# Later mixing splits, later gate-pair sums and a re-ordered second gate in a fused encoder-layer kernel

## Chip, core and metric

One core of a Trainium2 chip runs the whole layer as one program. The metric is the device time of one execution in microseconds (us): 1302.18 as the median of three runs before the change (1301.49 to 1302.49). Lower is better.

## What is computed

One layer of an encoder on 256 positions of width 2048, all in float32: a projection `P = RMSNorm(x) @ w_in` whose columns are gMLP u and v, attention q, k, v, and two gates; then two branches, a gated merge, an output projection, and a convolutional gated MLP. Cut to what matters here:

```python
uv, qkv, gates = split(rms_norm(x) @ w_in)
y_a = u * (w_s @ LN(v) + b)              # per 128-position chunk, 8 groups of 128 columns
y_b = neighbourhood_attn(q, k, v, rpb)   # 16 heads, learned relative bias
g_a, g_b = split(sigmoid(gates))         # 2048 columns each
merged = g_a * (y_a @ Wb_A) + g_b * (y_b @ Wb_B)
x = x + merged @ w_out
up = depthwise_conv(rms_norm(x) @ w_up)
x = rms_norm(x + (silu(gate) * val) @ w_down)
```

## The kernel before

**Products.** Every matrix product is made from values split in two: `whi` is the weight copied into a reduced format by ScalarE (L170, ACT), `wlo` is the remainder that VectorE subtracts (L171, DVE). Three matmuls (high by high, low by high, high by low; L250 to L252, or L317 to L319 in `triple`) make one product tile in a PSUM bank; there are 8 banks of 128x512.

**Pieces.** The program is a list of *pieces*, one for 256 rows of a weight block (512 columns). For each piece `begin(i)` runs in program order: it issues the DMA of piece i+4 on SyncE's queue (SP; five `wraw` buffers), lets ACT and DVE split piece i+3 (four `whi` and `wlo` buffers), and then runs the tasks that were put down for piece i with `at(i, f)`; TensorE (PE) then gets piece i's matmuls. Each engine works its own instructions off in this order, so the piece at which a task is put down decides what stands ahead of it on ACT, on DVE, on SP's queue and on GpSimd's (POOL).

**Mixings.** After each of the two groups of u columns, `mix(g)` (L690) runs at four pieces in a row: 4 matmuls with `w_s` (L693), two bias additions (L697) and a product with u (L698) on DVE. Its result `ya` (one buffer) is split by `end_mix`: ACT copies the high part (L536), DVE subtracts the low part (L537). `mix` begins with `end_mix` for the one before, and puts an `end_mix` at the next piece; that task stands behind the next `mix` of the same piece, so the second, third and fourth result of a group of four are split in the piece in which they are made. The second four run during the columns of the first q and k block (`g_at[0]`); at that block's end `combine` (L680 ACT, L682 DVE) and `spread` (L746, L747 DVE; L753 to L755 ACT) prepare the first two heads, and `attend` sends their scores to PE (L828).

**Heads.** `attend(hp, i)` spreads a pair of heads over ten pieces: scores at i, exponentials (L851, ACT) at i+1, weights (L859, ACT) at i+3, the turning of the weights on PE (L868) at i+5, their product with v (L878) at i+8. The last pair runs beside the first branch products (`g_at[8]`, `g_at[9]`).

**Wide products with sums.** The second halves of the two gates (`g_gw[0]`, `g_gw[1]`) are made by `run_wide` with a seven-product scheme: for certain pairs of pieces ("quads") 7 products in place of 8, from sums of activations and sums of weights. For a quad whose first piece is i, `wide` puts down: at i-3 the weight sums (L363, L364, L360, L361, DVE), at i-2 their split (L374 ACT, L375 DVE), at i-4 a read of the activation sums from DRAM (L1224, POOL queue). For a *kept* pair (`GATE_SPLIT`) the split weight sums were made early in the kernel and lie in DRAM; they are read back on the POOL queue (L1216) in two halves, "13" and "24", and the plain part of the pair is loaded at half width. `GATE_SPLIT[br] = {pair: (lead of the activation sums, lead of "13", lead of "24")}`. `GATE_ORDER[br]` is the order of the 16 row blocks, `GATE_QUADS[br]` says which pairs of that order are quads. Activation sums that are not at hand (`GATE_MADE`) are made by `sums_job` (L1312 and L323 to L326 on DVE; a piece later L1317 ACT and L1318 DVE; then a write to DRAM, L1322, POOL queue); for the last of them the piece is `g_at[8][1] + GATE_LATE`, and its buffer is closed after `g_m[0]`, at piece 12 of that count.

**The start of the second gate.** Its 16 pieces are called n0 to n0+15 below. The first gate's last results come off PSUM in `post_sums` (L590 to L594) and `add_sums` (L599); its sigmoid is L924 (ACT, with a table load ahead of it). At piece n0+2 `turn_m` turns a merged block on PE (L957) into two banks, which ACT (L962, L526) and DVE (L531) must empty before two of the four banks of the second gate's first quad can be written. That quad is also at n0+2, since position 0 of `GATE_QUADS[1]` is left out.

Of the kernel before, what the change touches and what calls it, by code (L numbers as in the profile page):

```python
# [50 lines left out]
X_SUMS = ((1, 5, 6), (2, 12, 13), (6, 18, 19))  # L51
GATE_KEPT, GATE_MADE = (1, 2, 6), (0, 3, 4)
GATE_QUADS = ((0, 1, 2, 4, 5, 6), (1, 2, 4, 5, 6))
GATE_ORDER = ((2, 3, 0, 1, 4, 5, 10, 11, 12, 13, 6, 7, 8, 9, 14, 15), (10, 11, 0, 1, 2, 3, 14, 15, 4, 5, 6, 7, 12, 13, 8, 9))
GATE_SPLIT = ({0: (4, 6, 5), 3: (4, 6, 6)}, {0: (4, 6, 6), 3: (4, 6, 6)})
GATE_FIRST = (40, (44, 46, 48, 48), (49, 51))
GATE_JOB = (3, (6, 6, 7, 7), (9, 12))
GATE_SUMS = ((0, 38, 40, "y4", "y5"), (3, 39, 40, "y6", "y7"))
GATE_LATE, Y_LATE = 4, 44
KEEP_AT = (22, 25, 29)  # L60
OUT_PAIRS = (0, 1, 2, 3, 4)
OUT_SUMS = (1, 3, 6, 9, 13)
# [16 lines left out]
def trunk_kernel(ctx, tc, x, x_t, vecs, w_in, ln_g, ln_b, w_st, b_s, rpb, w_branch, w_out, w_up, w_down,  # L79
# [26 lines left out]
    def bank():  # L106
        return psum.tile([128, 512], F32, name="bank")
# [81 lines left out]
    def at(i, f):  # L189
        tasks.setdefault(i, []).append(f)  # L190

    cur = [0]
# [91 lines left out]
    def wide(src, row0, order, c0, acts, quads, room, done, sums=None, stored=None, split=None, late=False):  # L284
        n0 = plan_wide(src, row0, order, c0)
        boxes = {}
        for q in quads:
            i = n0 + 2 * q
            k = order[2 * q]
            units[i], units[i + 1] = 1, 2  # L290
            b = boxes[q] = {}
            ready = split[0].get(k // 2) if split else None
            if stored:
                b["acts"] = {}
                at(i - (ready[0] if ready else 4), lambda b=b, k=k: stored(k // 2, b["acts"]))
            else:
                b["acts"] = sums[k]
            if ready:
                halved.add(i)
                for n, lead in zip(("13", "24"), ready[-2:]):  # L300
                    at(i - lead, lambda b=b, k=k, n=n: split[1](k // 2, b, n))
                continue
            whole[i] = whole[i + 1] = None
            halves = late and q == quads[0]
            at(i - 3, lambda i=i, b=b, halves=halves: weight_sums(i, b, room, halves))
            if halves:
                at(i - 2, lambda b=b: b.pop("rest")())
            at(i - 2, lambda b=b: weight_sums_split(b, room))
        return ("wide", n0, order, acts, quads, boxes, done)
# [225 lines left out]
    def split_plain(p, dst):  # L535
        nc.scalar.activation(dst[:, 0, :], p, AF.Copy)  # L536
        nc.vector.tensor_sub(dst[:, 1, :], p, dst[:, 0, :].bitcast(F32))  # L537
# [119 lines left out]
    def ev_u(j):  # L657
        def done(ps, i):
            G = gm_pool["p"]
            if j == 0:  # L660
                gm_pool["u"] = [G.tile([128, T], F32, name=f"u{b}") for b in range(8)]
            us = combine(ps)
            for b in range(4):
                nc.vector.tensor_mul(us[b], us[b], st1["rb"])

            def act():
                for b in range(4):
                    nc.scalar.activation(gm_pool["u"][j * 4 + b], us[b], AF.Gelu_apprx_tanh)

            at(i + 1, act)  # L670
            for b in range(4):
                at(i + 3 + b, lambda g=j * 4 + b: mix(g))
        return done
# [12 lines left out]
    def end_mix():  # L686
        gm_pool.pop("last", lambda: None)()

    def mix(g):
        end_mix()  # L690
        p = bank()
        for t in range(NT):
            nc.tensor.matmul(p[:, t * 128:(t + 1) * 128], gm_pool["v"][t][:, g * 128:(g + 1) * 128],  # L693
                             gm_pool["wsT"][:, g, :], start=True, stop=True)
        y = gm_pool["p"].tile([128, T], F32, name="ya", bufs=1)
        for t in range(NT):
            nc.vector.tensor_add(y[:, t * 128:(t + 1) * 128], p[:, t * 128:(t + 1) * 128], gm_pool["bs"][:, g, :])  # L697
        nc.vector.tensor_mul(y, y, gm_pool["u"][g])  # L698
        gm_pool["last"] = lambda: split_plain(y, yT[g])
        at(cur[0] + 1, end_mix)  # L700

    at_pool = {}

# [203 lines left out]
    def ev_gate_sums(br):  # L907
        def done(P, i):
            def go():
                gate_tile(br)  # L910
                mg["x", br] = [[mg["t", br][:, t, c * 512:(c + 1) * 512] for c in range(2)] for t in range(NT)]
                post_sums(P, mg["x", br], junk)

            at(i + 1, go)
        return done

    def ev_gate_wide(br):
        def done(ps, i):
            g = mg["t", br]
            add_sums(ps, mg["x", br])  # L920

            def sigmoid():
                for t in range(NT):
                    nc.scalar.activation(g[:, t, :], g[:, t, :], AF.Sigmoid, scale=st1["r"][:, t:t + 1])  # L924

            at(i + 1, sigmoid)
            for c in range(2):
                mg[br, 2 + c] = g[:, :, c * 512:(c + 1) * 512]
        return done
# [244 lines left out]
    def sums_room(name, dt):  # L1174
        return s_room["p"].tile([128, 2, 512], dt, name=name)
# [35 lines left out]
    def split_read(kept, g, tile_of):  # L1211
        def read(pair, box, n):
            u = box.setdefault("u", [])
            u.append([tile_of(pair, p + n) for p in "hl"])
            for t, src in zip(u[-1], kept[pair, g][n]):
                nc.gpsimd.dma_start(t.bitcast(F32), src)  # L1216
            if len(u) == 2:
                split_sums(box, u)
        return read

    def kept_sums(pair, box):
# [4 lines left out]

    g_gw = [wide(w_in2, 0, GATE_ORDER[br], (GA0, GB0)[br] + 1024, xt, GATE_QUADS[br], sums_room,
                 (ev_gate_sums(br), ev_gate_wide(br)), stored=kept_sums,
                 split=(GATE_SPLIT[br], split_read(g_kept, br, lambda pair, name: sums_room("k" + name, F32R))))
            for br in range(2)]  # L1230
# [41 lines left out]
    def split_rows(name, pair, g):  # L1272
        return {m: [dram.tile([128, 2, 512], F32, name=f"{name}_{h}{m}_{pair}_{g}") for h in "hl"]
                for m in ("13", "24")}
# [10 lines left out]
    for n, (pair, g) in enumerate((pair, g) for g in range(2) for pair in OUT_SPLIT[g]):  # L1285
# [3 lines left out]
                    [i + a for a in OUT_JOB[2]], 4, last=True)  # L1289
    for n, (pair, br) in enumerate((pair, br) for br in range(2) for pair in GATE_SPLIT[br]):  # L1290
        g_kept[pair, br] = split_rows("gate", pair, br)
# [261 lines left out]
```

## Time and profile before

| what | value |
|---|---|
| median of three runs | 1302.18 us |
| the profiled execution's own time | 1302.41 us |
| its span, first to last instruction | 1300.6 us |
| mean granted TensorE clock | 0.996 |
| PEld, DVE, ACT, POOL busy | 84%, 88%, 63%, 14% of the span |
| DMA: bytes, mean rate | 370.56 MB, 285 GB/s |

Rows of the profile give the line of the kernel, the engine, the operation, and `out<-in` by tile names. In a list of waits the columns are: engine and line that waited, whom for, us in total, how often, longest. In a timeline the first two columns are the start and the duration in us, and a bracket tells how long the engine had been idle and what ended that.

### The profile page before, as it was taken

What the parts mean: (1) busy time and instruction counts of PE and PEld (TensorE: products, weight loads), DVE (VectorE), ACT (ScalarE), POOL (GpSimd) and SP (SyncE); (2) the same over time, 40 slices, a digit from 0 to 9 for tenths busy, and PEclk for the clock granted to TensorE, in tenths of its full rate; (3) what the DMA queues carried; (4) which work ended last, traced back from release to release, by engine and by line L of the source; (5) the groups of instructions that cost most, each with busy time, mean ns of one, the idle gap of its engine ahead of it and who ended that gap; (6) DMA issues with size and microseconds to landing.
All of it is one profiled execution on the core that took longest, in us unless ns stands there. A gap on an engine that the chain in (4) does not pass through costs nothing.

```text
span 1300.6 us, 19691 instructions
## 1 busy us (share of the span) xinstructions
PE 1285.2 (99%) x6656; PEld 1094.2 (84%) x6656; DVE 1140.3 (88%) x1707; ACT 813.2 (63%) x1228; POOL 186.1 (14%) x336
## 2 busy tenths in 40 slices
PE   9999999999999999999999999999999999999997
PEld 7888878888788788888888888888888888888885
DVE  7898878888889788997898899899988989989988
ACT  7766577877855645466665656656565656555654
POOL 0004606334011001100001001100000001211210
PEclk9999999999999999999999999999999999999999
DMA  9789779998789876975688788789777859998993
GB/s 368 268 275 293 259 240 304 321 315 300 274 325 375 312 264 209 407 257 162 188 280 264 249 295 302 250 264 310 251 220 228 271 177 354 369 389 318 364 382 141
DMA packets 200181, 370.56 MB, mean 285 GB/s; under 512 B 16016, under 2 KB 124176, under 8 KB 200080
## 3 DMA queue, kind: packets, MB, share of 16 engines
q1 hardware_dynamic: 171728, 272.86, 61.5%
q0 software_dynamic: 27776, 95.39, 20.7%
q8 instruction: 52, 0.85, 0.3%
q10 hardware_dynamic: 576, 1.06, 0.2%
q14 instruction: 49, 0.40, 0.1%
HBM read 321.53 MB, written 45.61 MB: 282 GB/s over the span
## 4 chain that ended last, share of the span: by engine, by line
PE 64%; DVE 1%; DMA 1%; issue 0%; ACT 0%; DVEq 0%; SPq 0%
PE bank L222 24%; PE bank L226 13%; PE bank L319 8%; PE bank L317 8%; PE bank L318 8%; PE bank L251 1%; PE bank L250 1%; PE bank L252 1%; DMA wraw<-in_w_down_dram 1%; DVE wlo L171 1%; PE bank L1032 0%; DVE h L375 0%; PE bank L957 0%; DVE h L364 0%; ACT x L1158 0%
## 5 line engine op out<-in xcount | busy, mean ns | idle before, releaser
L171 DVE TENSOR_TENSOR wlo<-wraw,whi 128x1024 fp32r<-128x1024 f32 (+1 forms) x472 | 537.4, 1151 | 111.5 <-ACT whi L170 78.0
L170 ACT ACTIVATE whi<-wraw 128x1024 fp32r<-128x1024 f32 (+1 forms) x472 | 463.0, 996 | 186.6 <-PE bank L318 70.7
L222 PE MATMUL bank<-h,whi 128*128 128x512 f32 x1760 | 425.6, 392 | 0.0
L222 PEld LDWEIGHTS bank<-h,whi 128*128 128x128 f32 x1760 | 322.3, 188 | 61.6
L226 PEld LDWEIGHTS bank<-h,wlo 128*128 128x128 f32 x1760 | 225.9, 191 | 8.8
L226 PE MATMUL bank<-h,wlo 128*128 128x256 f32 x1760 | 228.7, 283 | 0.0
L1058 ACT ACTIVATE tc<-ta,ck 128x256 f32<-128x256 f32 x86 | 47.1, 595 | 110.2 <-DVE ta L1056 110.2
L317 PE MATMUL bank<-whi,h 128*128 128x512 f32 x192 | 75.5, 393 | 0.0
L319 PE MATMUL bank<-wlo,h 128*128 128x512 f32 x192 | 75.3, 392 | 0.2
L318 PE MATMUL bank<-whi,h 128*128 128x512 f32 x192 | 75.3, 392 | 0.0
L319 PE MATMUL bank<-wlo,a 128*128 128x512 f32 x188 | 73.5, 391 | 0.5 <-DVE wlo L171 0.5
L317 PE MATMUL bank<-whi,a 128*128 128x512 f32 x188 | 73.2, 390 | 0.0
L318 PE MATMUL bank<-whi,a 128*128 128x512 f32 x188 | 73.2, 389 | 0.0
L1061 DVE SCALAR_TENSOR_TENSOR tc<-ta,ck,tc 128x255 f32<-128x255 f32 x86 | 41.4, 481 | 14.4 <-ACT tc L1058 14.4
L1260 POOL DMA_DIRECT2D down_h<-so x16 | 8.7, 544 | 311.7 <-ACT so L1255 208.6
L793 POOL TENSOR_SCALAR_AFFINE_SELECT bias<-run 64x128 f32<-64x128 f32 x64 | 39.0, 642 | 90.8 <-DVE sc L836 90.1
L250 PE MATMUL bank<-whi,y 128*128 128x512 f32 x128 | 50.5, 395 | 0.0
L250 PE MATMUL bank<-whi,h 128*128 128x512 f32 x128 | 50.4, 394 | 0.0
L252 PE MATMUL bank<-wlo,h 128*128 128x512 f32 x128 | 50.0, 390 | 0.0
L252 PE MATMUL bank<-wlo,y 128*128 128x512 f32 x128 | 49.9, 390 | 0.0
L251 PE MATMUL bank<-whi,y 128*128 128x512 f32 x128 | 49.9, 390 | 0.0
L251 PE MATMUL bank<-whi,h 128*128 128x512 f32 x128 | 49.9, 390 | 0.0
(327 smaller groups left out, 2078.7 us busy)
## 6 DMA issues: line engine op xcount, KB each, us to landing
wraw<-in_w_up_dram SPq DMA_DIRECT2D x336, 256.0 KB, 4.1
wraw<-in_w_in_dram SPq DMA_DIRECT2D x107, 512.0 KB, 6.4
wraw<-in_w_down_dram SPq DMA_DIRECT2D x78, 512.0 KB, 7.7
wraw<-in_w_in_dram SPq DMA_DIRECT2D x70, 256.0 KB, 5.6
wraw<-in_w_branch_dram SPq DMA_DIRECT2D x32, 512.0 KB, 5.7
wraw<-in_w_out_dram SPq DMA_DIRECT2D x28, 512.0 KB, 5.9
h<-sums POOLq DMA_DIRECT2D x18, 512.0 KB, 7.8
tw<-in_w_down_dram POOLq DMA_DIRECT2D x8, 1024.0 KB, 9.0
```

What stands on the lines that cost most here:

```text
L170: nc.scalar.activation(h[:, k, :m], w[:, k, :m], AF.Copy)
L171: nc.vector.tensor_sub(l[:, k, :m], w[:, k, :m], h[:, k, :m].bitcast(F32))
L222: nc.tensor.matmul(p, h[:, k - k0, b * 128:(b + 1) * 128], acts(k), start=k == 0, stop=k == nk - 1)
L226: nc.tensor.matmul(p[:, :T], l[:, k - k0, b * 128:(b + 1) * 128], acts(k)[:, 0, :], start=False, stop=False)
L250: nc.tensor.matmul(p, xh, h[:, kk, :m], start=st, stop=False)
L251: nc.tensor.matmul(p, xl, h[:, kk, :m], start=False, stop=False)
L252: nc.tensor.matmul(p, xh, l[:, kk, :m], start=False, stop=sp)
L317: nc.tensor.matmul(p, xh, h, start=st, stop=False)
L318: nc.tensor.matmul(p, xl, h, start=False, stop=False)
L319: nc.tensor.matmul(p, xh, l, start=False, stop=sp)
L1058: nc.scalar.activation(v, u, AF.Identity, scale=ck[:, 1, ch:ch + 1], bias=ck[:, 3, ch:ch + 1])
L1061: nc.vector.scalar_tensor_tensor(v[:, 1:], u[:, :T - 1], ck[:, 0, ch:ch + 1], v[:, 1:], op0=OP.mult, op1=OP.add)
```

## The change

Three edits, all to what stands where; no instruction is added or taken away.

```diff
-GATE_ORDER = ((2, 3, 0, 1, ...), (10, 11, 0, 1, 2, 3, 14, 15, 4, 5, 6, 7, 12, 13, 8, 9))
-GATE_SPLIT = ({0: (4, 6, 5), 3: (4, 6, 6)}, {0: (4, 6, 6), 3: (4, 6, 6)})
+GATE_ORDER = ((2, 3, 0, 1, ...), (10, 11, 2, 3, 0, 1, 14, 15, 4, 5, 6, 7, 12, 13, 8, 9))
+GATE_SPLIT = ({0: (4, 6, 5), 3: (4, 6, 6)}, {0: (4, 7, 5), 3: (5, 4, 4)})
...
-GATE_LATE, Y_LATE = 4, 44
+GATE_LATE, Y_LATE = 7, 44
...
         gm_pool["last"] = lambda: split_plain(y, yT[g])
-        at(cur[0] + 1, end_mix)
+        if g % 4 == 3:
+            at(cur[0] + 1, end_mix)
```

The added line shifts all lines behind it by one; the rows of the changed program below carry the new numbers (L1256 for L1255, L860 for L859, and so on).

**Mixings.** Only the last `mix` of four puts down an `end_mix`; the others are split by the `end_mix` at the head of the next `mix`, one piece later. DVE, at the second four mixings (`u_1265` to `u_1267` are the u columns of groups 5 to 7, `y_1161` and `y_1162` the split results), before:

```order
L698 TENSOR_TENSOR ya<-ya,u_1265 128x256
L537 TENSOR_TENSOR y_1161<-ya,y_1161 128x256
L171 TENSOR_TENSOR wlo<-wraw,whi 128x1024
L697 TENSOR_TENSOR ya<-bank,bsb 128x128 x2
L698 TENSOR_TENSOR ya<-ya,u_1266 128x256
L537 TENSOR_TENSOR y_1162<-ya,y_1162 128x256
L171 TENSOR_TENSOR wlo<-wraw,whi 128x1024
```

and in the changed program:

```order
L698 TENSOR_TENSOR ya<-ya,u_1265 128x256
L171 TENSOR_TENSOR wlo<-wraw,whi 128x1024
L537 TENSOR_TENSOR y_1161<-ya,y_1161 128x256
L697 TENSOR_TENSOR ya<-bank,bsb 128x128 x2
L698 TENSOR_TENSOR ya<-ya,u_1266 128x256
L171 TENSOR_TENSOR wlo<-wraw,whi 128x1024
L537 TENSOR_TENSOR y_1162<-ya,y_1162 128x256
```

The subtraction L537 has changed places with the weight split L171 behind it. On ACT the copy L536 likewise now stands behind the weight copy L170 of the next piece.

**Late sums.** `GATE_LATE` moves the sums of one pair from pieces 4 and 5 to pieces 7 and 8 of `g_at[8]`. ACT, at the last pair of heads (L1255 and L170 are weight splits, L859 the weights of that pair, `pT` its turned weights), before:

```order
L1255 ACTIVATE th_3983<-tw 128x1024
L170 ACTIVATE whi<-wraw 128x1024
L1317 ACTIVATE tw<-tw 128x512
L859 ACTIVATE sc<-sc,sm 128x128 x4
L170 ACTIVATE whi<-wraw 128x1024 x2
L869 ACTIVATE pT<-bank 128x512
L170 ACTIVATE whi<-wraw 128x1024 x3
```

and in the changed program:

```order
L1256 ACTIVATE th_3983<-tw 128x1024
L170 ACTIVATE whi<-wraw 128x1024
L860 ACTIVATE sc<-sc,sm 128x128 x4
L170 ACTIVATE whi<-wraw 128x1024 x2
L870 ACTIVATE pT<-bank 128x512
L170 ACTIVATE whi<-wraw 128x1024
L1318 ACTIVATE tw<-tw 128x512
L170 ACTIVATE whi<-wraw 128x1024 x2
```

The split of the sums has gone from ahead of the heads' weights to behind the copy of the turned weights. On DVE the five instructions of the sums stand three weight splits later, and now ahead of two merge products (L935).

**Second gate.** Pairs 0 (kept) and 1 change places: the first quad, at n0+2, is now pair 1, whose weights are summed and split on the spot, and kept pair 0 comes at n0+4, two pieces later. ACT, from the first gate's post sums (`g_46..`) to the turned block (`f_..`, `m_..`), before:

```order
L590 ACTIVATE g_4625<-bank 128x512
L170 ACTIVATE whi<-wraw 128x512
L170 ACTIVATE whi<-wraw 128x1024
L170 ACTIVATE whi<-wraw 128x512
L924 ACT_TABLE_LOAD
L924 ACTIVATE g_4625<-g_4625,n_r 128x1024 x2
L170 ACTIVATE whi<-wraw 128x1024
L374 ACTIVATE h_4721<-t_4695 128x1024
L374 ACTIVATE h_4725<-t_4696 128x1024
L962 ACTIVATE f_4734<-bank 128x512
L526 ACTIVATE m_4178<-bank 128x256 x2
```

and in the changed program:

```order
L590 ACTIVATE g_4621<-bank 128x512
L170 ACTIVATE whi<-wraw 128x512
L170 ACTIVATE whi<-wraw 128x1024
L374 ACTIVATE h_4677<-t_4645 128x1024
L374 ACTIVATE h_4681<-t_4646 128x1024
L170 ACTIVATE whi<-wraw 128x512
L925 ACT_TABLE_LOAD
L925 ACTIVATE g_4621<-g_4621,n_r 128x1024 x2
L170 ACTIVATE whi<-wraw 128x1024
L963 ACTIVATE f_4734<-bank 128x512
L526 ACTIVATE m_4178<-bank 128x256 x2
```

DVE at the same place, before:

```order
L171 TENSOR_TENSOR wlo<-wraw,whi 128x512
L599 TENSOR_TENSOR g_4625<-bank,g_4625 128x512 x4
L171 TENSOR_TENSOR wlo<-wraw,whi 128x1024
L171 TENSOR_TENSOR wlo<-wraw,whi 128x512
L363 TENSOR_TENSOR t_4695<-wraw 128x512
L364 TENSOR_TENSOR t_4695<-wraw 128x512
L360 TENSOR_TENSOR t_4696<-t_4695,wraw 128x512
L361 TENSOR_TENSOR t_4696<-wraw,t_4696 128x512
L171 TENSOR_TENSOR wlo<-wraw,whi 128x1024
L375 TENSOR_TENSOR l_4722<-t_4695,h_4721 128x1024
L375 TENSOR_TENSOR l_4726<-t_4696,h_4725 128x1024
L531 TENSOR_TENSOR m_4178<-bank,m_4178 128x256 x2
```

and in the changed program:

```order
L171 TENSOR_TENSOR wlo<-wraw,whi 128x512
L363 TENSOR_TENSOR t_4645<-wraw 128x512
L364 TENSOR_TENSOR t_4645<-wraw 128x512
L360 TENSOR_TENSOR t_4646<-t_4645,wraw 128x512
L361 TENSOR_TENSOR t_4646<-wraw,t_4646 128x512
L599 TENSOR_TENSOR g_4621<-bank,g_4621 128x512 x4
L171 TENSOR_TENSOR wlo<-wraw,whi 128x1024
L375 TENSOR_TENSOR l_4678<-t_4645,h_4677 128x1024
L375 TENSOR_TENSOR l_4682<-t_4646,h_4681 128x1024
L171 TENSOR_TENSOR wlo<-wraw,whi 128x512
L171 TENSOR_TENSOR wlo<-wraw,whi 128x1024
L531 TENSOR_TENSOR m_4178<-bank,m_4178 128x256 x2
```

The four weight sums have moved ahead of the additions L599, and the splits of the weight sums (L374, L375) no longer stand right ahead of the emptying of the turned banks (L526, L531). On the POOL queue the reads of pair 0's halves are issued 7 and 5 pieces ahead of its quad, with pair 1's activation sums between them, and pair 3's halves 4 pieces ahead of its quad in place of 6, behind its activation sums.

More of the change, by code (lines that the diff above doesn't have):

```diff
@@ L53 @@
 GATE_QUADS = ((0, 1, 2, 4, 5, 6), (1, 2, 4, 5, 6))
-GATE_ORDER = ((2, 3, 0, 1, 4, 5, 10, 11, 12, 13, 6, 7, 8, 9, 14, 15), (10, 11, 0, 1, 2, 3, 14, 15, 4, 5, 6, 7, 12, 13, 8, 9))
-GATE_SPLIT = ({0: (4, 6, 5), 3: (4, 6, 6)}, {0: (4, 6, 6), 3: (4, 6, 6)})
+GATE_ORDER = ((2, 3, 0, 1, 4, 5, 10, 11, 12, 13, 6, 7, 8, 9, 14, 15), (10, 11, 2, 3, 0, 1, 14, 15, 4, 5, 6, 7, 12, 13, 8, 9))
+GATE_SPLIT = ({0: (4, 6, 5), 3: (4, 6, 6)}, {0: (4, 7, 5), 3: (5, 4, 4)})
 GATE_FIRST = (40, (44, 46, 48, 48), (49, 51))
```

## Prediction

> **What bounds the kernel now.** I read the busy shares first, then the list of TensorE's waits, then the timeline around each wait.
>
> ```profile
> PE 1285.2 (99%) x6656; PEld 1094.2 (84%) x6656; DVE 1140.3 (88%) x1707; ACT 813.2 (63%) x1228; POOL 186.1 (14%) x336
> ```
>
> ```profile
> PE bank L317 <- DVE m L531: 2.9, 1, 2.9
> ...
> PE bank L828 <- ACT ks L755: 1.4, 2, 0.9
> PE bank L868 <- ACT sc L859: 0.6, 1, 0.6
> ```
>
> PE is busy 99% of the span, so an edit that moves no product can only win what PE waits, and only these three waits lie where the change moves something. The list counts idle time alone; the timeline gives what each place costs, from the start of the last matmul ahead of it to the start of the first one behind it, against a place without a wait. The order of PE's rows there: the three products, then scores or turns, then the products again.
>
> ```profile
> 169.25 0.39 PE L252 MATMUL bank<-wlo,h 128*128 128x512 f32 x1
> ...
> 172.77 0.43 PE L250 MATMUL bank<-whi,h 128*128 128x512 f32 x1
> ```
>
> ```profile
> 220.16 0.39 PE L252 MATMUL bank<-wlo,h 128*128 128x512 f32 x1
> ...
> 221.24 0.44 PE L250 MATMUL bank<-whi,h 128*128 128x512 f32 x1
> ```
>
> Scores of the first pair of heads take 172.77 - 169.25 = 3.52 us, those of a later pair 1.08: **2.44 us** are lost.
>
> ```profile
> 331.69 0.39 PE L252 MATMUL bank<-wlo,h 128*128 128x512 f32 x1
> ...
> 332.27 0.48 PE L250 MATMUL bank<-whi,y 128*128 128x512 f32 x1
> ```
>
> ```profile
> 353.01 0.39 PE L252 MATMUL bank<-wlo,y 128*128 128x512 f32 x1
> ...
> 354.98 0.49 PE L250 MATMUL bank<-whi,y 128*128 128x512 f32 x1
> ```
>
> The turning of the last pair takes 1.97 us, that of an earlier one 0.58: **1.39 us** are lost.
>
> ```profile
> 429.61 0.39 PE L319 MATMUL bank<-kl,s 128*128 128x512 f32 x1
> 432.90 0.47 PE L317 MATMUL bank<-kh,s 128*128 128x512 f32 x1 [2.90 <-DVE m L531]
> ...
> 434.13 0.49 PE L319 MATMUL bank<-kl,s 128*128 128x512 f32 x1
> ...
> 438.01 0.40 PE L317 MATMUL bank<-whi,s 128*128 128x512 f32 x1
> ```
>
> Matmuls of 512 columns start 0.227 us apart (a triple is 0.68 us), so the step from 429.61 to 432.90 loses 3.29 - 0.23 = **3.06 us**. The ten steps from 434.13 to 438.01 take 3.88 us in place of 2.27, which loses **1.61 us** more. Why, the windows by engine say (PE, PEld, DVE, ACT, POOL busy, then the granted clock):
>
> ```profile
> 430.90:434.30 3.40, 1.40 (x6) 1.21 (x7) 3.33 (x7) 3.40 (x8) 0.39 (x1) 1.00 0.28 74
> 434.29:437.70 3.41, 3.41 (x10) 2.67 (x9) 1.76 (x3) 0.75 (x2) 2.24 (x5) 0.50 0.72 250
> ```
>
> PE was busy for 1.40 us of one stretch of 3.40, and the granted clock is 0.50 for the 3.41 us behind it. The three places together lose 2.44 + 1.39 + 3.06 + 1.61 = 8.5 us, which is all that this change can win.
>
> **The mixings.** DVE and ACT while the second four mixings run:
>
> ```profile
> 158.60 0.48 DVE L697 TENSOR_TENSOR ya<-bank,bsb 128x128 f32<-128x128 f32 x2
> 159.12 0.42 DVE L698 TENSOR_TENSOR ya<-ya,u 128x256 f32<-128x256 f32 x1
> 160.02 0.42 DVE L537 TENSOR_TENSOR y<-ya,y 128x256 fp32r<-128x256 f32 x1 [0.48 <-ACT y L536]
> 160.97 1.22 DVE L171 TENSOR_TENSOR wlo<-wraw,whi 128x1024 fp32r<-128x1024 f32 x1 [0.53 <-ACT whi L170]
> ...
> 165.63 1.41 DVE L682 TENSOR_TENSOR ta<-bank,tb 128x256 f32<-128x256 f32 x4
> ```
>
> ```profile
> 159.57 0.42 ACT L536 ACTIVATE y<-ya 128x256 fp32r<-128x256 f32 x1 [2.15 <-DVE ya L698]
> ...
> 163.09 0.42 ACT L536 ACTIVATE y<-ya 128x256 fp32r<-128x256 f32 x1 [2.15 <-DVE ya L698]
> 164.36 0.91 ACT L680 ACTIVATE tb<-bank 128x256 f32<-128x256 f32 x3
> ...
> 170.09 0.41 ACT L755 ACTIVATE ks<-ta 64x256 fp32r<-64x256 f32 x1
> ```
>
> One mixing costs 163.09 - 159.57 = 3.52 us, in which DVE works 0.48 + 0.42 + 0.42 + 1.22 = 2.54: it waits for ACT's copy of a value that it has just made, and then for the weight copy that was stuck behind that copy. A gate piece of 12 matmuls takes PE 12 x 0.227 = 2.72 us, so the two engines fall behind, and PE pays at the first scores. With the split a piece later both waits have a whole piece of other work between maker and user; the cycle falls to DVE's 2.54 us, and three of the four mixings are shortened, by 0.98 us each. L682 comes 2.9 us earlier, and with it the chain to L755: ks is ready at 170.50 - 2.9 = 167.6, and PE would ask for it at 169.25 + 0.23 = 169.48. The cover is 1.9 us for the first half of the scores and less for the second, whose copies follow on the same engine, so I take all 2.44 us; the bounds are 0 (the wait stays, if the chain is held by something else than the copies) and 2.44. The moved splits themselves cost nothing: they are the same instructions on engines with time over, and the branch products that read them (`y`) start at 332.27.
>
> **The late sums.** ACT at the last pair of heads:
>
> ```profile
> 349.38 1.04 ACT L170 ACTIVATE whi<-wraw 128x1024 fp32r<-128x1024 f32 x1
> 353.04 0.63 ACT L1317 ACTIVATE tw<-tw 128x512 fp32r<-128x512 f32 x1 [2.62 <-DVE tw L326]
> 353.58 1.27 ACT L859 ACTIVATE sc<-sc,sm 128x128 f32<-128x128 f32 x4
> ```
>
> The copy of the sums idles for DVE 2.62 us, with the heads' weights queued behind it. Without it ahead, these can run from 350.42 to 351.7, and PE asks at 353.24: the 1.39 us go, with 1.5 us of cover. Where the sums go there is work enough: their five DVE instructions then delay two L935 merges by about 2 us, but these only empty two of eight banks and the next product groups (10.9 us each) take other banks. The write to DRAM is issued later as well:
>
> ```profile
> 355.04 0.58 POOL L1322 DMA_DIRECT2D xsums<-tw  x1 [43.64 <-DVE tw L1318]
> ```
>
> It moves by three pieces of 2.7 us, to about 363, piece 10 of this count. POOL's next reads (activation sums and kept weights of the first gate, from piece 12 on) stand behind it in the queue, and one of them reuses its buffer, so that read waits until the write has landed. Its product is at piece 18, eight pieces or 22 us behind the write, which holds a write and a read of about 8 us each. I count 0; bounds 0 and 2 us lost.
>
> **The second gate.** What stands ahead of the turned banks on ACT and DVE, and DVE's emptying of them:
>
> ```profile
> 423.47 0.63 ACT L170 ACTIVATE whi<-wraw 128x512 fp32r<-128x512 f32 x1 [1.66 <-PE bank L318]
> ...
> 425.42 2.19 ACT L924 ACTIVATE g<-g,n_r 128x1024 f32<-128x1024 f32 x2
> 427.52 1.04 ACT L170 ACTIVATE whi<-wraw 128x1024 fp32r<-128x1024 f32 x1
> 428.47 1.99 ACT L374 ACTIVATE h<-t 128x1024 fp32r<-128x1024 f32 x2
> ```
>
> ```profile
> 419.31 2.48 DVE L599 TENSOR_TENSOR g<-bank,g 128x512 f32<-128x512 f32 x4
> ...
> 432.01 1.41 DVE L531 TENSOR_TENSOR m<-bank,m 128x256 fp32r<-128x256 f32 x4
> ```
>
> Now pair 1's split weight sums go earlier: the 1.99 us of L374 fall into ACT's idle 1.66 us ahead of 423.47 and push what follows by 0.33. L924 ends at 427.94, the weight copy at 428.9, its subtraction on DVE (1.22) at 430.1, and the first two L531 (0.35 apart, 0.41 long) at 430.85 in place of 432.75. PE, released 0.15 us behind that today (432.90), goes on at 431.0 where it wants to at 429.61 + 0.23 = 429.84: **a wait of 1.2 us stays**, 3.06 - 1.2 = 1.86 us go. On DVE four weight sums of the size of L599 (2.48 us) now stand ahead of L599, which delays the first gate's banks by those 2.5 us to 424.3; PE turns into them at 426.3 (429.84 less four triples and eight transposes, twice the 0.35 us of the four above). The wait's bounds are 0 (ACT gets to its table load earlier than I think) and the 3.06 of today.
>
> With 1.2 us idle, PE is busy for over 2 of any 3.4 us. Around the first scores, which lost 2.44 us in two waits, the granted clock stays 1.00, so I take the half clock as gone: 1.61 us.
>
> [...]
>
> The kept reads: pair 3's halves share buffers with pair 0's, which PE now finishes one quad (seven triples, 4.8 us) later, and they are needed at the same place.
>
> ```profile
> wraw<-in_w_in_dram SPq DMA_DIRECT2D x11, 512.0 KB, 7.9
> ...
> kl<-gate_l POOLq DMA_DIRECT2D x4, 512.0 KB, 7.2
> ```
>
> Between them lie eight triples (5.4 us), pair 2's quad (4.8) and three triples (2.0): 12 us for a landing of 7.2 (the median between 405 and 440 us). I count no wait; with a landing of 14 it would be 2.
>
> **Sum.** 2.44 + 1.39 + 1.86 + 1.61 = 7.3 us off the profiled execution's 1302.41 gives 1295.1; the median of the runs is 0.2 lower, so **1295.0**.
>
> **Rivals.**
> - *The half clock stays*, because 1.2 us idle at an unlucky place, or something else, lets it fall. Gain 5.7, time 1296.7. For it: the trace has one fall only. Against: no fall at 172 us. 0.13.
> - *Another wait takes L531's place* and nothing is won at the second gate: the copy behind the table load, or the late L599, holds the turned banks as long. Gain 3.83, time 1298.6. 0.09.
> - *The first scores still wait*, since DVE, late by its split jobs and not by the copies, comes no earlier. Gain 4.9, time 1297.5. For it: DVE is 88% busy. 0.05.
> - *Little is won anywhere*: half of the 2.44 and the 1.39, about 1300.2. The order shows that the rows did move, so this needs two failures. 0.07.
> - *Slower: the second piece of pair 1 lands late.* Its raw weights are now needed for the sums (L364) at about 420, not six us later for another pair. It is issued as
>
> ```profile
> 411.76 0.33 SPq L145 DMA_DIRECT2D wraw<-in_w_in_dram  x1
> ```
>
>   and with 7.9 us lands at 419.7. Up to about 420.6 ACT's chain covers it; every us behind that moves L599, the weight split and L531 by one. PE's wait is then 1.2 + (landing - 420.6); with the half clock's 1.61 it passes today's 4.67 plus the 3.83 won elsewhere from a landing at 426.3, 14.5 us behind the issue, and is slower by 0.2% from 428.9. At 20 us (431.8) the wait is 12.4 and the time 1302.4 + 12.4 + 1.6 - 8.5 = 1307.9. Twice the measured landing; 0.06.
>
> **Chances and range.** Forecast 0.60. About 0.2% (2.6 us) is what a measurement can tell from no change: faster by more means below 1299.6, which the forecast and the first three rivals give: 0.87; the fourth counts as the same, 0.07; slower 0.06. The range goes from 1293.4 (all 8.5 us back, 0.3 for the runs' spread) to 1298.7 (nothing at the second gate), and leaves out 0.13.
>
> **What would show it.** Right: in PE's list of waits the rows for L828 and L868 are gone, L317's is about 1.2 us, the clock is 1.00 throughout, the first scores take 1.08 us and the last turning 0.58, L536 no longer idles for L698. Wrong: a row for L828 with another releaser, a wait for L364 or L375 at the second gate, a wait of PE for `kh` or `kl`, or a stretch at 0.50 behind L317.

## The result, and the profile after

The changed kernel takes **1294.24 us** (median of four runs, 1294.04 to 1294.45), the kernel before beside it 1302.34 (1301.49 to 1303.07): ratio 0.9938, 95% interval 0.9921 to 0.9955, 8.1 us less. The profiled execution takes 1294.45 us with a span of 1292.7 and a mean granted clock of 0.998. Lines of the changed program are one higher behind L700.

The busy shares, and then TensorE's whole list of waits in the changed kernel:

```profile
PE 1282.1 (99%) x6656; PEld 1092.4 (85%) x6656; DVE 1140.8 (88%) x1707; ACT 813.8 (63%) x1228; POOL 189.1 (15%) x336
```

```profile
PE bank L493 <- DVE one L483: 1.5, 1, 1.5
PE bank L317 <- ACT m L526: 0.8, 1, 0.8
```

The shares say nothing: PE is at 99% as before. The list says it: the rows for the scores and for the last turning are gone, and the 2.9 us at the second gate have become 0.8. (Why this row names L526 and not L531 is told with the reasons below. L493 is in the start of the program, alike in both kernels.) The three places, in TensorE's timeline of the changed kernel:

```profile
169.44 0.39 PE L252 MATMUL bank<-wlo,h 128*128 128x512 f32 x1
...
170.52 0.44 PE L250 MATMUL bank<-whi,h 128*128 128x512 f32 x1
```

```profile
350.78 0.39 PE L252 MATMUL bank<-wlo,y 128*128 128x512 f32 x1
351.01 0.60 PE L869 MATMUL bank<-ident,sc 128*128 128x128 f32 x4
351.36 0.48 PE L250 MATMUL bank<-whi,y 128*128 128x512 f32 x1
```

```profile
425.98 0.39 PE L319 MATMUL bank<-l,s 128*128 128x512 f32 x1
427.13 0.47 PE L317 MATMUL bank<-h,s 128*128 128x512 f32 x1 [0.76 <-ACT m L526]
...
428.05 0.47 PE L317 MATMUL bank<-h,s 128*128 128x512 f32 x1
...
428.82 0.40 PE L317 MATMUL bank<-h,h 128*128 128x512 f32 x1
```

First scores: 1.08 us, the price of any later pair. Last turning: 0.58 us, likewise. Second gate: the step over the wait is 1.15 us, of which 0.92 are lost, and no stretch of half clock follows. The next six steps, from 427.13 to 428.82, take 1.69 us in place of 1.36, so 1.25 us are lost here in all; half of the further 0.33 is a short wait for the second turned bank at 428.05, too short for the list. In the 3.41 us around the wait (columns as before: PE, PEld, DVE, ACT, POOL busy, each with its number of instructions, then the clock, the DMA share and GB/s) PE was busy for 2.65 us:

```profile
424.53:427.94 3.41, 2.65 (x12) 1.66 (x10) 2.80 (x6) 3.41 (x9) 0.00 (x0) 1.00 0.70 214
```

The programs have the same 6656 matmuls in nearly the same order, so each can be paired with its twin of before, and the shift of the start times read place by place. That gives the account that the medians can't give (median shift of PE's matmuls at 150, 180, 362, 420, 450 and 1295 us, and from these the change within each stretch; negative is earlier; e1 to e9 are the experiments below; each figure holds to some 0.01 us, and the start of the program differs by up to 0.2 us between executions):

| change of PE's start, us | first scores | last turning | second gate | 450 us to the end |
|---|---|---|---|---|
| changed kernel | -2.43 | -1.39 | -3.53 | -0.82 |
| e1, mixings alone | -2.42 | +2.42 | +1.24 | -0.83 |
| e2, late sums alone | +0.05 | -1.39 | -0.31 | -0.80 |
| e3, second gate alone | +1.77 | +0.63 | -3.52 | -0.82 |
| e4, mixings and late sums | -2.43 | -1.39 | -0.02 | -0.79 |
| e9, changed kernel, turned block a piece earlier | -2.43 | -1.39 | -4.82 | -0.78 |

The three edits account for 2.43 + 1.39 + 3.53 = 7.35 us. The last column belongs to none of them: before's profiled execution waits 0.47 us for a weight split (L171) in the last product, near 1283 us, which the other six executions of the table do not, and two further executions (e5, e7) wait in the last product again with the change in.

### The profile page after: what moved, and what is told of

Same layout as the page of the kernel before. It is cut to its first block, busy times and chain, and to the rows that moved or that the text cites. A ratio compares the mean times of both kernels' runs of the same rounds, so it can differ in the third digit from the quotient of the medians.

```text
span 1292.7 us, 19683 instructions
## 1 busy us (share of the span) xinstructions
PE 1282.1 (99%) x6656; PEld 1092.4 (85%) x6656; DVE 1140.8 (88%) x1707; ACT 813.8 (63%) x1228; POOL 189.1 (15%) x336
## 4 chain that ended last, share of the span: by engine, by line
PE 99%; ACT 0%; DMA 0%; DVE 0%; issue 0%; ACTq 0%
PE bank L222 31%; PE bank L226 16%; PE bank L317 12%; PE bank L319 12%; PE bank L318 12%; PE bank L250 5%; PE bank L252 5%; PE bank L251 4%; PE bank L829 1%; PE bank L879 0%; DMA xr<-in_x_t_dram 0%; PE bank L693 0%; PE bank L869 0%; PE bank L1033 0%; PE bank L958 0%; ACT g L925 0%
## 5 line engine op out<-in xcount | busy, mean ns | idle before, releaser
L171 DVE TENSOR_TENSOR wlo<-wraw,whi 128x1024 fp32r<-128x1024 f32 (+1 forms) x472 | 538.1, 1152 | 105.4 <-ACT whi L170 71.7
L170 ACT ACTIVATE whi<-wraw 128x1024 fp32r<-128x1024 f32 (+1 forms) x472 | 463.4, 996 | 194.9 <-PE bank L318 77.5
```

The costliest lines, as they stand in the source:

```text
L170: nc.scalar.activation(h[:, k, :m], w[:, k, :m], AF.Copy)
L171: nc.vector.tensor_sub(l[:, k, :m], w[:, k, :m], h[:, k, :m].bitcast(F32))
```

## The experiments

**One edit at a time.** The theory: three separate waits, each removed by its own edit, and a half clock that the second gate's wait brings about. The rivals: the edits need each other (a wait shrinks only once the engines are ahead), or a new wait takes the old one's place.

*e1, the mixings alone*, before with

```diff
-        at(cur[0] + 1, end_mix)
+        if g % 4 == 3:
+            at(cur[0] + 1, end_mix)
```

> The kernel before with the mixing edit alone. If the three edits act apart, the first scores take 1.08 us in place of 3.52 and the time falls by 2.4 us; the wait of 2.9 us at the second gate stays, only 2.4 us earlier. Whether the half clock behind it stays depends on where the windows of 3.41 us lie: with the windows where they were in the profile of before, the whole wait falls into one of them and the half clock stays. Rival: DVE is late by its split jobs, the first scores still wait, under 0.5 us is won.

Measured: 1299.69 us (eleven runs, 1297.3 to 1303.2), ratio 0.9965 [0.9952, 0.9977]. TensorE's waits in it:

```profile
PE bank L317 <- DVE m L531: 2.9, 1, 2.9
...
PE bank L869 <- ACT sc L860: 1.5, 1, 1.5
```

The scores' wait is gone and the whole 2.42 us with it, so the copies held that chain. But the profiled execution, at 1302.67 us the second slowest of the eleven, pays all of it back at the last turning, where the wait has grown from 0.6 to 1.5 us. ACT in e1, 74 us ahead of that wait, says why:

```profile
277.00 1.06 ACT L170 ACTIVATE whi<-wraw 128x1024 fp32r<-128x1024 f32 x1 [0.82 <-DMA wraw<-in_w_in_dram]
```

A weight block landed late. From there ACT and DVE are 1.73 us earlier than before, PE 2.57, and the 0.84 us between them stay until the last turning, PE's next wait for the two. In e4, whose ACT has no such wait at this place, ACT and DVE keep their 2.44 us. Here, then, what was won ahead of a wait was kept only as far as the weights landed earlier, too.

The rest of the +2.42, some 1.6 us, is the clock. The stretches of e1 ahead of and behind the two half clocks:

```profile
350.19:353.60 3.41, 1.96 (x9) 1.00 (x8) 2.75 (x6) 2.29 (x6) 0.29 (x1) 1.00 0.91 317
353.60:357.01 3.41, 3.41 (x10) 2.63 (x9) 2.92 (x3) 1.88 (x3) 0.29 (x1) 0.50 0.94 306
428.69:432.11 3.41, 1.15 (x6) 0.61 (x4) 3.41 (x4) 3.41 (x8) 0.00 (x0) 1.00 0.47 155
432.11:435.52 3.41, 2.77 (x7) 2.22 (x8) 3.35 (x6) 2.13 (x3) 1.04 (x2) 0.50 0.04 5
435.52:438.93 3.41, 3.41 (x10) 2.64 (x9) 0.58 (x2) 0.63 (x1) 1.57 (x3) 0.50 0.92 334
```

A wait of 1.5 us was enough for a fall, and in the stretch at half clock behind it 8 matmuls begin, where 15 do at full clock. (The x10 of the row counts those that reach in from the stretch before or are cut by an edge, too.) Behind the gate's wait two stretches at 0.50 follow in place of before's one: that is the +1.24 of the table.

*e2, the late sums alone*, before with

```diff
-GATE_LATE, Y_LATE = 4, 44
+GATE_LATE, Y_LATE = 7, 44
```

> The kernel before with the late sums alone. If the edits act apart, the last turning takes 0.58 us in place of 1.97 and the time falls by 1.4 us; the scores' 2.44 us and the second gate's wait stay. Rival: the sums behind the heads delay the first gate's reads and give back what is won: no difference, and a new wait of PE between 355 and 400 us.

Measured: 1300.14 us (nine runs, 1298.6 to 1303.45), ratio 0.9972 [0.9961, 0.9983]. The last turning gives its 1.39 us and no wait comes up behind it. The other two waits stay:

```profile
PE bank L317 <- DVE m L531: 2.9, 1, 2.9
...
PE bank L828 <- ACT ks L755: 1.4, 2, 1.0
```

The median falls by more than 1.39 us; the next part tells why medians of these kernels can't be read to a microsecond.

*e3, the second gate alone*, before with the new `GATE_ORDER[1]` and `GATE_SPLIT[1]`:

> The kernel before with the second gate's order and reads alone. If the edits act apart, PE's step at the second gate loses 0.9 us in place of 3.06 and no half clock follows: 3.7 us faster (2.1 from the wait, 1.6 from the clock). Rival: the wait shrank in the changed kernel only because PE came earlier to it by the other two edits; then the wait stays near 2.9 us here and nothing is won.

Measured: 1300.29 us (eleven runs, 1298.71 to 1304.23), ratio 0.9973 [0.9962, 0.9984]. Its waits:

```profile
PE bank L828 <- ACT ks L755: 1.7, 2, 1.3
...
PE bank L868 <- ACT sc L859: 1.3, 1, 1.3
PE bank L317 <- ACT m L526: 0.8, 1, 0.8
```

The gate's wait is the 0.8 us of the changed kernel, without the other edits: its 3.52 us come from this edit alone, and the rival that the edits need each other falls. The last turning loses 0.63 us more than in before, as in e1: at 345 us ACT and DVE run 2.25 us later than in before and PE only 1.58, since a weight block landed 0.67 us late at 232 us. In this execution the half clock has moved to the first scores:

```profile
168.81:172.23 3.41, 1.62 (x8) 0.90 (x6) 2.60 (x7) 2.87 (x7) 0.00 (x0) 1.00 0.71 244
172.23:175.64 3.41, 3.41 (x10) 2.74 (x11) 2.63 (x4) 2.81 (x3) 0.00 (x0) 0.50 0.09 16
```

*e4, mixings and late sums without the second gate*, the changed kernel with the old `GATE_ORDER[1]` and `GATE_SPLIT[1]`:

> The changed kernel with the second gate's edit undone. If the edits act apart, 3.8 us faster than before, with the wait of 2.9 us still at the second gate, 3.8 us earlier. If the half clock goes by what share of a window is idle, and the windows lie as in the profile of before, the wait is split 1.3 to 1.6 between two windows and the clock stays at 1.00: then 5.4 us faster. If any wait of 2.9 us brings the half clock: 3.8 us.

Measured: 1297.97 us (five runs, 1297.83 to 1298.89), ratio 0.9953 [0.994, 0.9966]. Only the gate's wait is left, at its full length:

```profile
PE bank L317 <- DVE m L531: 2.9, 1, 2.9
```

The two edits give 2.43 + 1.39 in the trace and the gate nothing: a stretch with 0.50 us of PE work and one at half clock behind it are there. The median lies 5.5 us below before's, close to the 5.4 that were expected without a fall; the profiled execution, with 1297.93 us as good as the median, has the fall, so those 5.5 us are no sign of its absence. Together e3 and e4 show that the parts add up, where they are counted place by place.

**When the clock falls.** In all eleven profiled executions of this study the granted clock changes only on a grid of 3.41 us, whose phase differs (its first edge lies 4.2 to 6.9 us behind the span's start). In before the clock's record begins at 4.21 us, and the clock falls at 434.29, rises at 437.70 and falls again at 1294.44: 126, 127 and 378 steps of 3.413 us behind the first edge. The fall to 0.50 at the end of every program, where PE has run out of work, lies on the grid as well. On this grid, the stretches at full clock with the least PE work and the clock behind them; those with no PE work at all, at the programs' ends, are left out, and a fall follows behind each of them (from 2.5 us on the second row names only two of several):

| PE busy in the stretch of 3.41 us | clock in the next |
|---|---|
| 0.50 (e4), 1.13 (e2), 1.15 (e1), 1.39 (before), 1.62 (e3), 1.96 (e1); at the end of the program 0.19 (e6), 0.37 (e1), 1.35 (before), 1.36 (e5) | 0.50 |
| 2.12 (e3), 2.34 (e2), 2.41 (before), 2.53 (before), 2.65 (changed kernel); at the end of the program 1.49 (e9), 1.70 (e4), 1.73 (e7), 1.86 (e3), 2.24 (e2) | 1.00 |

The highest that fell is quoted above (e1 at 350.19), and so is the 2.65 of the changed kernel. The lowest that did not fall is e9's, in which PE's last work ends at 1283.06; the stretch behind it, without any PE work, is still at 1.00. Before's scores, which lost 2.44 us in two waits, stayed above, too:

```profile
1281.57:1284.98 3.41, 1.49 (x7) 0.91 (x5) 3.07 (x8) 2.29 (x7) 0.00 (x0) 1.00 0.52 197
1284.98:1288.39 3.41, 0.00 (x0) 0.00 (x0) 1.67 (x6) 1.12 (x2) 0.00 (x0) 1.00 0.66 249
```

```profile
168.07:171.48 3.41, 2.41 (x11) 1.54 (x10) 2.61 (x6) 2.33 (x5) 0.00 (x0) 1.00 0.88 303
```

So a stretch with 2.12 us or more never brought a fall and one with 1.39 or less always did; between 1.49 and 1.96 both came about. PE's busy time is thus not quite what decides. The row of a matmul of 512 columns is 0.39 us long while the next one starts 0.227 us behind it, and one of 128 columns (a turn, L868 in before) 0.28 us, while four turns take 0.35 us from the first to the next product (331.69 to 332.27 less 0.23). So a row is longer than the step it adds, most of all a short one, and where nothing follows the whole row counts as busy. An estimate from the same traces: if every matmul counts with 0.227 us per 512 columns, at the end of its row, e1's 1.96 becomes 0.97 and e3's 1.62 becomes 0.91, while e9's stays 1.49, and all falls lie at 1.36 or less, all others at 1.49 or more. That count was fitted afterwards; no run tests it.

In before the scores' two waits (0.92 and 0.46 us) fell into two stretches, in e3 (1.26 and 0.46) into one, and e3's waits were longer as well. At its unluckiest, a stretch of 3.41 us would hold 1.87 us of work over before's scores (169.56 to 172.97), in the range where falls came about, but 2.65 us over the wait that the changed kernel still has (426.28 to 429.69). So whether a place like before's scores costs its wait, or its wait and more, depends, as far as these traces tell, on where the grid lies in that execution. Where a fall came behind a wait in the middle of the program, it cost from 1.3 us (e2's gate) over 1.6 (before's) to 2.9 us (e1's, with two stretches). The spread of the runs points the same way. Beside e1 to e4 the kernel before ran 26 times, from 1301.97 to 1307.81 us, and the mean clock of its runs from 0.999 down to 0.993: the three at 0.993 and 0.994 took 1306.17 to 1307.81, the two at 0.998 and 0.999 1302.41 and 1302.78, and the rest 1301.97 to 1305.16. It isn't the only spread: the runs of e9, which waits nowhere in these places, still differ by 2 us. The first four runs of the changed kernel are all at 0.998 and within 0.4 us; six later ones (e8) are at 0.998 or 0.999 and spread over 1.3 us. The medians of the single edits hold these draws, so they do not add up: their gains against before's 1303.43 in that batch, 3.74 + 3.29 + 3.14, make 10.2 us, against 8.1 for the change as a whole in the first batch. The change itself is worth 9.6 us in the batch of e8, where before took 1304.27.

**What of the second gate's edit matters.** *e5* keeps the new order of pairs, but reads both halves of pair 0 at once again, 6 pieces ahead, and pair 3's activation sums 4 pieces ahead:

```diff
-GATE_SPLIT = ({0: (4, 6, 5), 3: (4, 6, 6)}, {0: (4, 7, 5), 3: (5, 4, 4)})
+GATE_SPLIT = ({0: (4, 6, 5), 3: (4, 6, 6)}, {0: (4, 6, 6), 3: (4, 4, 4)})
```

> The changed kernel with both halves of pair 0 read 6 pieces ahead again and pair 3's activation sums 4 pieces ahead, so only the pair order is changed and the reads are not spread. If the reads have time over either way, as their leads of 12 us and more say, the time is that of the changed kernel within 0.3 us. Rival: the spread is what lets pair 1's activation sums land in time; then PE waits at the second gate's first quad for s, and the time is 1 us or more above the changed kernel.

Measured: 1294.94 us (1294.16 to 1295.98), ratio 0.9933 [0.992, 0.9945]. Its waits:

```profile
PE bank L319 <- DVE wlo L171: 1.3, 2, 0.8
```

The gate's wait is the changed kernel's 0.8 us. No product waits for a kept half (`kh`, `kl`) or an activation sum (`s`); the two waits for L171 lie at 12 and at 1276 us, far from the gate, and up to 450 us PE is where the changed kernel's is (-7.08 against -7.16). The order of the pairs does it, and spreading those reads adds nothing that shows. The time itself, 0.7 us above the changed kernel's first runs and 0.25 above e8's, is not fine enough to say so, and the 0.3 us expected were missed against the first. Pair 3's halves stay at 4 pieces ahead here, so their later read, which the prediction ties to the buffers that they share with pair 0, was not tried by itself.

**What is left of the wait.** *e6* turns the merged block one piece earlier, at n0+1, in the changed kernel:

```diff
-                at(i + 1 if j == 3 else g_gw[1][1] + 2 if j == 1 else i + 2, lambda: turn_m(j))
+                at(i + 1 if j == 3 else g_gw[1][1] + 1 if j == 1 else i + 2, lambda: turn_m(j))
```

> The changed kernel with the turning of the merged block one piece earlier, at n0+1, so that the turned banks are emptied ahead of the sigmoid's table load and of the next weight split. If what is left at the second gate (0.92 us) is the queue on ACT and DVE ahead of L526 and L531, PE does not wait there any more and the time is 0.9 us below the changed kernel. Rival: the turning then waits itself for the first gate's banks, which L599 empties 2.5 us later than before the change, and nothing is won or up to 1 us lost.

Measured: 1292.84 us (1292.69 to 1293.74), ratio 0.9917 [0.9903, 0.9931]. The gate's wait is gone, and nothing waits for L599 in its place. Since this version is faster than both kernels, it ran once more, as *e9*, beside the changed kernel, *e8*, on one chip, five rounds each.

> The changed kernel itself, measured beside the next one. If the turned block's place is worth what the first runs of the two gave apart: this kernel takes 1294.0 to 1294.6 us, its mean clock 0.998. If no half clock falls in any of its executions, its runs lie within 0.5 us of each other, while those of the kernel before, which falls in some, spread over several us.

> The kernel of e6_turn once more, beside the changed kernel on the same chip. If the last wait of the second gate (0.92 us) and the emptying of the turned banks behind it are what was left: 1.0 to 1.6 us below the changed kernel, 1292.6 to 1293.2 us, only the short wait for the first gate's post sums (L483) left among the waits of the TensorE banks. If the first figure was luck of the runs: within 0.4 us of the changed kernel.

Measured: e8 1294.69 us (1294.21 to 1295.53), ratio to before 0.9929 [0.9915, 0.9943]; e9 **1293.32 us** (1292.98 to 1294.95), ratio 0.9921 [0.9907, 0.9935], 1.4 us below e8. Both ratios are to before, whose runs spread over 6 us, so the two intervals overlap; the two medians and the traces are the better evidence: at the gate PE is 4.82 us earlier than before in e9, 3.53 in the changed kernel. These 1.29 us are the whole 1.25 that were lost there, not the 0.92 of the first step alone. The expectations were missed in part: the medians of e8 and e9 each lie 0.1 us above the range given, and e8's runs spread over 1.3 us and not 0.5, though none of them has a mean clock under 0.998; e9 also has a wait of 0.31 us for a weight split at 11.9 us, far from the change. ACT in e9 at the place where the changed kernel waits:

```profile
419.89 0.61 ACT L170 ACTIVATE whi<-wraw 128x512 fp32r<-128x512 f32 x1
420.42 0.60 ACT L963 ACTIVATE f<-bank 128x512 f32<-128x512 f32 x1
...
421.92 0.69 ACT L526 ACTIVATE m<-bank 128x256 fp32r<-128x256 f32 x2
422.63 1.28 ACT L925 ACT_TABLE_LOAD   x1
```

and in the changed kernel:

```profile
419.99 0.61 ACT L170 ACTIVATE whi<-wraw 128x512 fp32r<-128x512 f32 x1
420.62 1.28 ACT L925 ACT_TABLE_LOAD   x1
421.92 2.19 ACT L925 ACTIVATE g<-g,n_r 128x1024 f32<-128x1024 f32 x2
424.01 1.04 ACT L170 ACTIVATE whi<-wraw 128x1024 fp32r<-128x1024 f32 x1
424.96 0.58 ACT L963 ACTIVATE f<-bank 128x512 f32<-128x512 f32 x1
425.44 0.64 ACT L526 ACTIVATE m<-bank 128x256 fp32r<-128x256 f32 x2
```

The turned banks are emptied ahead of the table load and the sigmoid instead of behind them. What was left of the wait was thus the queue that begins with ACT's table load, and the sigmoid, now 2 us later, holds up nothing that shows in PE's list of waits.

**Where the late sums must stand.** *e7* puts them at pieces 5 and 6 in place of 7 and 8:

```diff
-GATE_LATE, Y_LATE = 7, 44
+GATE_LATE, Y_LATE = 5, 44
```

> The changed kernel with the late sums at pieces 5 and 6 in place of 7 and 8: the split of the sums still stands behind the heads' weights on ACT, but now ahead of the copy of the turned weights. If only the place behind the weights counts, the time is that of the changed kernel within 0.3 us and PE has no wait at the last pair of heads. Rival: the copy of the turned weights is then late behind the sums and the products with v wait: up to 1 us lost.

Measured: 1294.37 us (1293.96 to 1295.29), ratio 0.9929 [0.9917, 0.9942], no wait at the last turning, the gate's 0.8 us as in the changed kernel. Behind the heads' weights is what counts; between pieces 5 and 7 no difference shows.

## Why the prediction was right

Forecast 1295.0, measured 1294.24: the likeliest case came about, with all three mechanisms. (The sum gives 1294.9: 1295.1 less 0.2.) How near the medians come is in part luck of the runs, since the same change is worth 8.1 us in the first batch and 9.6 in that of e8; the account by place is the better test.

- **First scores, 2.44 us, all taken**: 2.43. A mixing's cycle was put at DVE's 2.54 us; DVE's L698 now stand 2.45 and 2.52 apart, with no wait for ACT between them:

```profile
155.40 0.42 DVE L698 TENSOR_TENSOR ya<-ya,u 128x256 f32<-128x256 f32 x1
...
157.85 0.42 DVE L698 TENSOR_TENSOR ya<-ya,u 128x256 f32<-128x256 f32 x1
158.19 1.22 DVE L171 TENSOR_TENSOR wlo<-wraw,whi 128x1024 fp32r<-128x1024 f32 x1
159.33 0.42 DVE L537 TENSOR_TENSOR y<-ya,y 128x256 fp32r<-128x256 f32 x1
...
160.37 0.42 DVE L698 TENSOR_TENSOR ya<-ya,u 128x256 f32<-128x256 f32 x1
...
162.18 1.41 DVE L682 TENSOR_TENSOR ta<-bank,tb 128x256 f32<-128x256 f32 x4
```

  L682 comes 3.45 us earlier; 2.9 were predicted. The cover was a little larger than thought.
- **Last turning, 1.39 us**: 1.39. The cover was smaller than the 1.5 us given: with the DMA wait of 0.95 us that this execution, too, has at 277 us, the heads' weights (L860) end at 350.29, 0.7 us ahead of PE's 351.01. The write to DRAM, put at about 363 us in before's times, was issued at 358.64, which with the 3.63 us that PE is ahead here is 362.3; the next read waited 1.78 us for it on POOL's queue, and PE did not wait for that read, as counted. The write and the read were put at about 8 us each; before's medians from issue to landing are 7.4 us for the write and 11.2 for reads of activation sums, together 18.6 of the 22 us that were counted on.

```profile
349.03 1.26 ACT L860 ACTIVATE sc<-sc,sm 128x128 f32<-128x128 f32 x4
```

```profile
358.64 0.58 POOL L1323 DMA_DIRECT2D xsums<-tw  x1 [48.55 <-DVE tw L1319]
...
365.17 0.53 POOL L1225 DMA_DIRECT2D s<-xsums  x1 [1.78 <-DMA xsums<-tw]
```

- **Second gate, "a wait of 1.2 us stays"**: 0.92 us stayed in the step over the wait, so 2.14 of the 3.06 went in place of 1.86. The path was the one given, from the table load over the weight copy and its subtraction to L531, each about 0.2 us earlier. The row of the wait names L526, but the first two L531 end at 426.98 and the next two at 427.90 (rows below), and PE goes on 0.15 us behind each of them (427.13 and 428.05), as it does in before (432.75 and 432.90). L599 was put at 424.3 in before's times; it ends at 420.68 (row below), which with the 3.63 us that PE is ahead is 424.3.
- **Half clock, 1.61 us**: gone. The wait and the half clock together were put at 1.86 + 1.61 = 3.47; PE gained 3.53 there. The nearness is a balance of small errors: the first step kept 0.28 us less than predicted, and the next six kept 0.33 us that the sum didn't have, with 0.1 us behind the wait of before that it didn't count either. Of the two reasons given, one held: 1.2 us of idle time leave PE over 2 us of work in any stretch of 3.41 (2.65 at the least, with the wait as it came out), and no stretch with 2.12 or more fell. The other, "around the first scores, which lost 2.44 us in two waits, the granted clock stays 1.00", is no reason: in e3, with waits only 0.34 us longer in sum, the same place fell, so that before's did not was at least in part the luck of that execution's grid.
- **The first rival, the half clock that stays, did not come about**: the changed kernel's clock is 1.00 from the start of its record, 4.69 us behind the span's start, to 1288.10 us, where PE has had no work since before 1284.69:

```profile
1284.69:1288.10 3.41, 0.00 (x0) 0.00 (x0) 3.09 (x9) 2.03 (x5) 0.00 (x0) 1.00 0.78 296
1288.10:1291.51 3.41, 0.00 (x0) 0.00 (x0) 0.00 (x1) 0.11 (x1) 0.00 (x0) 0.50 0.81 308
```

- **No wait in L531's place, no late second piece of pair 1**: DVE in the changed kernel runs the four weight sums without a gap, so the raw weights for L364 had landed by 416.28. The slower rival needed a landing later than 426.3, which is 422.7 in the times of this execution.

```profile
415.68 0.68 DVE L363 TENSOR_TENSOR t<-wraw 128x512 f32<-128x512 f32 x1
416.28 0.69 DVE L364 TENSOR_TENSOR t<-wraw 128x512 f32<-128x512 f32 x1
...
418.21 2.47 DVE L599 TENSOR_TENSOR g<-bank,g 128x512 f32<-128x512 f32 x4
...
426.23 0.75 DVE L531 TENSOR_TENSOR m<-bank,m 128x256 fp32r<-128x256 f32 x2
427.14 0.76 DVE L531 TENSOR_TENSOR m<-bank,m 128x256 fp32r<-128x256 f32 x2 [0.16 <-ACT m L526]
```

- The sum of the terms was 7.3 us; 7.35 came from the edits, and the other 0.8 of the difference of the profiled executions from the last product, which the change does not touch.

## What to carry to other kernels

An instruction that waits for a value made just now held up what stood behind it on its engine (before's ACT idled 2.62 us for DVE's sums at L1317, with the heads' weights queued behind): put the use one piece of work behind the making, and put work without a deadline (late sums, a sigmoid with its table load) behind the instruction that TensorE waits for. Count a change place by place, by the shift of each matmul against its twin, where the medians may carry half clocks of some executions (before's runs have mean clocks from 0.993 to 0.999). TensorE waits that leave under some 2 us of work in a stretch of 3.41 us cost up to 2.9 us more than themselves here where the clock fell, so a wait is worth shortening even where it can't be removed.

## What the runs showed of the hardware

- The clock fell after every stretch of the 3.41 us grid with 1.39 us of PE work or less, and never after one with 2.12 or more; between 1.49 and 1.96 us both came about. What exactly is counted stays open; the count by columns given above would put the bound between 1.36 and 1.49 us. That this sets the spread of before's runs is inferred from their mean clocks; each label has the trace of one execution only.
- The recovery isn't settled either: after a fall, a stretch with 2.77 us of PE work at half clock (e1, above) was followed by another at 0.50, and one with 2.79 (e2) by full clock.

```profile
427.61:431.02 3.41, 1.13 (x5) 0.59 (x4) 3.41 (x4) 3.41 (x8) 0.00 (x0) 1.00 0.54 186
431.02:434.43 3.41, 2.79 (x7) 2.24 (x8) 3.35 (x6) 2.12 (x3) 1.04 (x2) 0.50 0.02 6
```

- In e2 the wait reaches into the stretch at 0.50, and the fall cost 1.3 us in place of before's 1.6: PE only resumed 0.6 us into the stretch, and six matmuls from there took 2.70 us in place of 1.36.
- In some executions ACT waits 0.8 to 0.95 us for a weight block at 277 us (e1, the changed kernel), in others not (before, e4). PE does not wait there, but ACT and DVE run later for the next 75 us by as much (in the changed kernel from 2.23 us ahead of before to 1.32).
